# Prompt attention of a hybrid decoder step as one pipeline across units, the cache copies paced from later on, and a ring buffer with a fourth slot

## Chip, cores and metric

One Trainium2 chip, one of its cores. The metric is the time of one execution on the device in microseconds (us). TensorE (PE, its weight loads PEld), VectorE (DVE), ScalarE (ACT), GpSimd (POOL) and SyncE (SP) each work through their own queue in order; SP, POOL and ACT also issue DMAs.

## The reference, cut to what matters

One layer of a decoder runs over a prompt of 1024 rows and 64 sample rows (8 streams of 8), with shared weights. Branch A is a gated depthwise convolution of width 31, branch B dilated window attention in 3 groups of 8 heads; the groups' outputs are weighted by the softmax of their denominators. The sample rows attend to caches, and the caches are also returned, shifted by 8 rows.

```
h = x @ w_in + b_in      # [conv value | conv gate | z_a | q | k | v (3 groups each) | z_b | g_a | g_b]
c = silu(layernorm(causal_conv31(a_val * sigmoid(a_gate)) + conv_b))
for g, (window, d) in enumerate(((128, 1), (512, 4), (2048, 16))):
    o[g], lse[g] = softmax_attention(q[g], k[g], v[g])     # keys t, t-d, ..., t-window, ALiBi penalty
attn = sum_g softmax_g(lse)[g] * o[g]
m = sigmoid(g_a) * (c * silu(z_a)) @ w_a + sigmoid(g_b) * (attn * silu(z_b)) @ w_b
y = layernorm(alpha * x + m @ w_out)
outputs: y, the groups' new k and v of the prompt, the sample caches shifted by 8 rows, the conv state
```

## The kernel before

Every projection is a sum of three products: x and the weights are split into a high and a low part (`split`, lines 100 and 101: ACT writes `hi`, DVE writes `lo`, from a `raw` that SP loads), and L171 multiplies hi by hi, hi by lo and lo by hi, in column chunks of 384, 352 and 352. One 128-column slice of weights is 72 such products. `raw`, `hi` and `lo` have two buffers each. The values' projection (`project_v`, L269) works on 512 columns, from weights `vhi` and `vlo` in four pieces of 512 KB.

**Prompt attention** runs over 12 units, one for each pair of heads f (0 to 3) and group g (0 to 2). `project_qk` of unit u+2 and `project_v` are written between units; a timeline simulation inside the scheduler sets each engine's order, by priorities. A unit is cut into bursts (4, 3 or 2 by group, 36 in all). For a burst PE computes scores S (L322, 4 or 8 products on half of the array's rows), DVE adds the bias and takes the row extremum (L332), ACT takes the exponential P in place (L349), PE transposes P in blocks of 128 (L359), DVE and ACT copy the transposes out of PSUM (L367, L365), PE multiplies them with the values (O, L376, on half of the array's columns), and the result is copied to `og` (L394, L392). The first transpose of a burst waits for its last exponential, and the first score of a burst for the last reduction of the burst before. Between a unit's bursts PE is given projection products.

After each f, `combine` makes the weights of the three groups: small DVE operations, a transpose on PE (L435), a store to DRAM on POOL (`wd`), six loads that spread its rows over the partitions (`wb`, POOL, L444), and multiplications on DVE (L446, L448, L449). The convolution (`conv`, L495 and L497 on DVE) has low priority.

**Copies.** The shifted caches are 88 copies from DRAM to DRAM, issued by ACT: 64 of 1020 KB, then 16 of 1008 KB, then 8 of 480 KB. `pace` issues them after the split of a weight, `credit[1]` copies for each: 1.7 from `project_qk(0)` on, 0 in the sample stage, 1.25 after it. 74 of them are issued in the prompt phase, 14 in the stage of the last gates.

**Sample stage.** Four passes load keys and values of the caches (8, 4 and 1 loads of 512 KB for keys, as many for values) through a ring of slots `kvs`: 0, 1, 2, and from pass 0's values on also 9, 10, 11 (six). Scores are L619, L627 and L631 (the last: group 0's keys, one load `g1k`), values L664, L672 and L678. 24 gate projections (L709) are spread over this and the next stage, and stored to DRAM (`sgb`, `sga`, `sza`). Slots 9 to 11 hold `og` of the last f until its `combine` has read them; slot 5 holds keys of a unit.

**Late stages.** After the convolution's normalisation and the projection of z_b, `w_b` (8 weights of 256 KB) is multiplied; meanwhile `sza` comes back in 24 pieces through two buffers `sb` (L808), each multiplied on DVE (L827) and split into the x slots by ACT and DVE; `w_a` needs all of them. Then w_a, w_out (L875) and the last layer norm.

## Time and profile before

| | |
|---|---|
| median of 3 runs | 1440.72 us (1439.12 to 1442.24) |
| the profiled execution | 1443.81 us |
| its span on the core | 1441.8 us |
| mean granted TensorE clock | 0.991 |
| PE busy | 1408.4 us (98%) |
| DVE, ACT, POOL busy | 843.0 us (58%), 447.0 us (31%), 173.2 us (12%) |
| DMA | 280.19 MB, mean 194 GB/s |

The span is what the profiler sees between the first and the last instruction; the profiled execution is 2 us longer than its span. Times of the rows below are from the span's start. A row of a timeline merges instructions that follow each other; "x8" counts records, and a score, value or transposing product has two records. "[0.25 <-issue]" is idle time ahead of the row, and what ended it.

### The profile page before, as it was taken

What the parts mean: (1) busy time and instruction counts of PE and PEld (TensorE: products, weight loads), DVE (VectorE), ACT (ScalarE), POOL (GpSimd) and SP (SyncE); (2) the same over time, 40 slices, a digit from 0 to 9 for tenths busy, and PEclk for the clock granted to TensorE, in tenths of its full rate; (3) what the DMA queues carried; (4) which work ended last, traced back from release to release, by engine and by line L of the source; (5) the groups of instructions that cost most, each with busy time, mean ns of one, the idle gap of its engine ahead of it and who ended that gap; (6) DMA issues with size and microseconds to landing.
All of it is one profiled execution on the core that took longest, in us unless ns stands there. A gap on an engine that the chain in (4) does not pass through costs nothing.

```text
span 1441.8 us, 22039 instructions
## 1 busy us (share of the span) xinstructions
PE 1408.4 (98%) x8656; PEld 1265.2 (88%) x8656; DVE 843.0 (58%) x1642; ACT 447.0 (31%) x997; POOL 173.2 (12%) x310
## 2 busy tenths in 40 slices
PE   8899999999999999998989999999999999999997
PEld 7788888899999999988877878897899999999885
DVE  4114132328959779497986886671357326535676
ACT  5205032133424434246421211212146422203210
POOL 1011111210111011103440601100000000000000
PEclk9999999999999999999999999999999999999999
DMA  7959477365666575753477665557854326535321
GB/s 249 325 191 339 154 254 257 100 206 169 201 220 195 172 227 177 229 193 113 141 243 268 254 253 210 195 201 307 300 190 145 130 71 200 176 91 166 106 101 59
DMA packets 91590, 280.19 MB, mean 194 GB/s; under 512 B 21632, under 2 KB 47552, under 8 KB 90080
## 3 DMA queue, kind: packets, MB, share of 16 engines
q1 hardware_dynamic: 76032, 151.62, 31.5%
q10 hardware_dynamic: 2816, 87.30, 17.3%
q0 software_dynamic: 12640, 39.88, 8.6%
q8 instruction: 68, 1.11, 0.3%
q14 instruction: 34, 0.28, 0.1%
HBM read 240.85 MB, written 125.20 MB: 254 GB/s over the span
## 4 chain that ended last, share of the span: by engine, by line
PE 44%; DMA 6%; DVE 2%; issue 0%; SPq 0%; ACT 0%; DVEq 0%
PE mm L171 32%; PE mm L875 7%; DMA sb<-sza 2%; DMA kv<-in_g2v_dram 2%; PE S L619 1%; DMA kv<-in_g1v_dram 1%; DMA raw<-in_w_in_dram 1%; DMA kv<-in_g1k_dram 1%; PE S L631 1%; PE S L627 1%; PE O L678 1%; DVE x L101 1%; PE O L664 0%; PE O L376 0%; DVE lo L101 0%
## 5 line engine op out<-in xcount | busy, mean ns | idle before, releaser
L171 PE MATMUL mm<-x,hi 128*128 128x352 f32 (+1 forms) x3648 | 915.8, 331 | 7.3 <-ACT x L100 4.8
L171 PEld LDWEIGHTS mm<-x,hi 128*128 128x128 f32 x3648 | 644.7, 189 | 37.6 <-issue 24.6
L171 PE MATMUL mm<-x,lo 128*128 128x352 f32 (+1 forms) x1824 | 602.1, 330 | 0.4 <-DVE lo L101 0.4
L171 PEld LDWEIGHTS mm<-x,lo 128*128 128x128 f32 x1824 | 343.6, 188 | 15.0 <-issue 13.0
L495 DVE SCALAR_TENSOR_TENSOR cv<-ub,conv_w,cv 128x1024 f32<-128x1024 f32 x240 | 307.7, 1282 | 1.9
L101 DVE TENSOR_TENSOR lo<-raw,hi 128x1024 fp32r<-128x1024 f32 (+2 forms) x87 | 98.8, 1135 | 130.1 <-ACT hi L100 130.1
L100 ACT ACTIVATE hi<-raw 128x1024 fp32r<-128x1024 f32 (+2 forms) x87 | 85.9, 987 | 251.5 <-PE mm L171 211.4
L269 PE MATMUL mm<-vhi,x 128*128 128x512 f32 x384 | 120.2, 393 | 5.4 <-ACT vhi L100 5.4
L349 ACT ACTIVATE P<-P,st 128x128 f32<-128x128 f32 (+1 forms) x192 | 84.2, 440 | 62.8 <-DVE st L332 62.4
L269 PEld LDWEIGHTS mm<-vhi,x 128*128 128x128 f32 x384 | 72.9, 190 | 20.9 <-ACT vhi L100 5.8
L709 ACT ACTIVATE gst<-mm,b_in 128x352 f32<-128x352 f32 (+1 forms) x72 | 40.1, 558 | 143.6 <-PE mm L171 114.9
L269 PE MATMUL mm<-vlo,x 128*128 128x512 f32 x192 | 75.3, 392 | 0.0
L270 DVE TENSOR_TENSOR vst<-mm,vb 128x512 f32<-128x512 f32 x24 | 16.6, 691 | 100.3 <-PE mm L269 100.3
L497 DVE SCALAR_TENSOR_TENSOR cv<-keep,conv_w,cv 128x64 f32<-128x64 f32 x240 | 68.8, 286 | 3.5
L332 DVE CUSTOM_DVE_ANT_0 P<-S,bias 128x128 f32<-128x128 f32 (+1 forms) x192 | 55.2, 350 | 22.8 <-PE S L322 22.8
L610 POOL COPY qf<-keep 64x16 f32<-64x16 f32 x96 | 55.9, 594 | 48.5 <-PE S L619 30.0
L875 PE MATMUL mm<-wol,mh 128*128 128x512 f32 (+1 forms) x144 | 56.1, 390 | 0.0
L875 PE MATMUL mm<-woh,mh 128*128 128x512 f32 (+1 forms) x144 | 56.1, 390 | 0.0
L875 PE MATMUL mm<-woh,ml 128*128 128x512 f32 (+1 forms) x144 | 56.0, 389 | 0.0
L359 PE MATMUL PT<-ident,P 128*128 128x128 f32 x280 | 41.8, 284 | 3.9 <-ACT P L349 3.9
L269 PEld LDWEIGHTS mm<-vlo,x 128*128 128x128 f32 x192 | 36.3, 189 | 7.7 <-issue 0.2
L100 ACT ACTIVATE vhi<-raw 128x1024 fp32r<-128x1024 f32 x12 | 12.7, 1057 | 93.1 <-PE mm L277 69.3
(184 smaller groups left out, 1311.6 us busy)
## 6 DMA issues: line engine op xcount, KB each, us to landing
out_nb_dram<-in_cache_dram ACTq DMA_DIRECT2D x64, 1020.0 KB
raw<-in_w_in_dram SPq DMA_DIRECT2D x67, 512.0 KB
kv<-in_g3k_dram SPq DMA_DIRECT2D x32, 512.0 KB
kv<-in_g3v_dram SPq DMA_DIRECT2D x32, 512.0 KB
out_nb_dram<-in_cache_dram ACTq DMA_DIRECT2D x16, 1008.0 KB
kv<-in_g2k_dram SPq DMA_DIRECT2D x16, 512.0 KB
kv<-in_g2v_dram SPq DMA_DIRECT2D x16, 512.0 KB
raw<-in_w_v_dram SPq DMA_DIRECT2D x12, 512.0 KB
```

What stands on the lines that cost most here:

```text
L100: h = act.activation(out=dst_hi, in_=src, func=AF.Copy)
L101: dve.tensor_tensor(out=dst_lo, in0=src, in1=dst_hi.bitcast(F32), op=ALU.subtract)
L171: pe.matmul(ps[:, :cn], a, b, start=(i == 0), stop=(i == len(ops) - 1))
L269: pe.matmul(ps, a, b, start=(i == 0), stop=(i == len(ops) - 1))
L332: last = dve.tensor_tensor_reduce(out=pr[:, h, c], in0=ps[:, h, c], in1=bias[:, h, b0:b0 + nk], scale=-1.0, scalar=3e38, op0=ALU.add, op1= ...
L349: ex = act.activation(out=pr[:, h, c], in_=pr[:, h, c], func=AF.Exp, scale=-1.0, bias=st[:, t, h, 0:1], accum_out=st[:, t, h, 1:2])
L359: m = pe.transpose(pp[:, i * P:(i + 1) * P], pr[:, h, c:c + P], ident)
L495: dve.scalar_tensor_tensor(out=acc[:, :NP_], in0=ub[:, j:j + NP_], scalar=w, in1=acc[:, :NP_], op0=ALU.mult, op1=ALU.add)
L497: dve.scalar_tensor_tensor(out=accs, in0=us[:, :, j:j + 8], scalar=w, in1=accs, op0=ALU.mult, op1=ALU.add)
L610: pool.tensor_copy(out=qfull(g)[hs, f].rearrange("p (r j h) -> p r j h", r=4, j=4)[:, :, :, 2 * f + h2], in_=qs[hs, g * 4 + f, 16 * pr:16 ...
L709: act.activation(out=st[:, c0:c0 + cn], in_=ps, func=func, bias=b_sb[:, f:f + 1])
L875: pe.matmul(ps[:n], a, b, start=(i == 0), stop=(i == len(ops) - 1))
```

## The change

It has three parts.

- **The row.** `visit` takes the place of the loop over bursts. Each call writes, at priority 700, one row: the transposes of the newest burst, the values of the burst before that, and the scores of the next burst. The values' and the scores' first product wait, by an added dependency, for the exponential that the transposes wait for too; the values also wait for the copy out of PSUM on ACT. The pipeline is not emptied between units; two calls after the last unit empty it. What follows a unit's last value (the copy to `og`, the store of its statistics) is written with the values.
- **The copies.** `credit[1] = 1.7` moves behind `project_qk(0)`, `project_qk(1)` and `project_v(0)`. The queue of copies is the same, so ten of them move from the prompt phase to later.
- **The ring.** `kvs` begins with slots 0, 1, 2 and 5, and has seven slots later.

```diff
+    pipe = []
+    def visit(burst=None):
+        with tc.high_priority(700):
+            gate = pipe[-1]["exp"] if pipe else None
+            if pipe and "pts" not in pipe[-1]:
+                transposes(pipe[-1])
+            if len(pipe) == 2 or burst is None:
+                values(pipe.pop(0), gate)
+            if burst:
+                scores(burst, gate)
+                pipe.append(burst)
+    def together(m, gate):
+        tc.add_manual_dep(m.ins, gate.ins.name, SYNC, reason="the row starts complete")
...
+                m = pe.matmul(ps[:, h, off[t]:off[t] + nb * P], q[hs, qc], k[hs, kc], start=True, stop=True)
+                if gate is not None:
+                    together(m, gate)
+                    gate = None
...
+                if i0 + i == 0:
+                    together(m, x["exp"])
...
+                    if first:
+                        together(m, x["evac"])
+                        if gate is not None and gate is not x["exp"]:
+                            together(m, gate)
+                        first = False
...
-                    with tc.high_priority(100):
-                        m = pe.matmul(ps[:, h, off[t]:off[t] + nb * P], q[hs, qc], k[hs, kc], start=True, stop=True)
-                    if last is not None:
-                        tc.add_manual_dep(m.ins, last.ins.name, SYNC, reason="the burst starts complete")
...
-        made = scores(BURSTS[g][0])
-        for bi, burst in enumerate(BURSTS[g]):
-            off, pr = made
-            if bi + 1 < len(BURSTS[g]):
-                made = scores(BURSTS[g][bi + 1])
...
+        un = {"g": g, "q": q, "k": k, "vt": vt, "scr": scr, "bias": bias, "st": st, "og": og, "tiles": qtiles(g)}
+        for b in BURSTS[g]:
+            visit({"unit": un, "tiles": b})
+        return og, st if g == 0 else scr
...
-    credit[1] = 1.7
...
     project_v(0)
+    credit[1] = 1.7
...
+    visit()
+    visit()
...
-    kvs = [0, 1, 2]
+    kvs = [0, 1, 2, 5]
```

The new lines of the same work are L331 (scores), L360 (transposes), L384 (values), L341 (reduction), L348 (exponential), L368 and L366 (copies of the transposes), L454 (transpose in `combine`), L465, L467 and L468 (its multiplications), L514 and L516 (convolution), L652 (scores of group 0's cache).

How the order moves is read at four places. **First, PE in the middle of a unit** of group 0 (mm are projection products, S scores, PT transposes, O values; "waits" names the engines waited for). Before:

```order
2342 L171 MATMUL mm_4149<-x_122,hi_4117 128x352
2343 L322 MATMUL S_3920<-qkv_3120,qkv_3119 128x256 [waits DVE_49]
2344 L322 MATMUL S_3920<-qkv_3120,qkv_3119 128x256 x3
2345 L171 MATMUL mm_4149<-x_130,hi_4117 128x352
2346 L359 MATMUL PT_3935<-ident_197,P_3889 128x128 [waits PE_49,Activation_49]
2347 L359 MATMUL PT_3935<-ident_197,P_3889 128x128
2348 L376 MATMUL O_3877<-PT_3894,vt_3836 64x128 [waits DVE_49]
2349 L376 MATMUL O_3877<-PT_3894,vt_3836 64x128 x7
2350 L359 MATMUL PT_3935<-ident_197,P_3889 128x128 x2
2351 L359 MATMUL PT_3941<-ident_197,P_3889 128x128 x4
2352 L171 MATMUL mm_4149<-x_122,lo_4118 128x352
```

The same place after:

```order
2332 L171 MATMUL mm_4108<-x_122,hi_4076 128x352
2333 L360 MATMUL PT_3872<-ident_197,P_3862 128x128 [waits PE_49,Activation_49]
2334 L360 MATMUL PT_3872<-ident_197,P_3862 128x128 x3
2335 L360 MATMUL PT_3878<-ident_197,P_3862 128x128 [waits DVE_49]
2336 L360 MATMUL PT_3878<-ident_197,P_3862 128x128 x3
2337 L384 MATMUL O_3884<-PT_3834,vt_3791 64x128 [waits DMAHW7_49,PE_49]
2338 L384 MATMUL O_3884<-PT_3834,vt_3791 64x128 x5
2339 L331 MATMUL S_3891<-qkv_3078,qkv_3077 128x256 [waits DVE_49]
2340 L331 MATMUL S_3891<-qkv_3078,qkv_3077 128x256 x3
2341 L171 MATMUL mm_4108<-x_130,hi_4076 128x352
```

Scores, transposes and values stood in separate groups, cut by each other and by projection products; now they stand in one row, the scores last. Over the whole program PE changes between its array shapes 257 times before and 226 times after, and 34 to 57 projection products stand between the scores of one row and the transposes of the next.

**Second, DVE at the third combine**, where its multiplications wait for `wb`. Before:

```order
680 L495 SCALAR_TENSOR_TENSOR cv_5228<-ub_5050,conv_w_203,cv_5228 128x1024 [waits DVE_49]
681 L446 TENSOR_TENSOR attn_5292<-og_3841,wb_5475 128x1024 [waits DMASW5_49,DMASW4_49]
682 L495 SCALAR_TENSOR_TENSOR cv_5228<-ub_5050,conv_w_203,cv_5228 128x1024 [waits DVE_49]
683 L448 TENSOR_TENSOR wb_5479<-og_4459,wb_5479 128x1024 [waits DMASW7_49,DMASW6_49]
684 L495 SCALAR_TENSOR_TENSOR cv_5228<-ub_5050,conv_w_203,cv_5228 128x1024 [waits DVE_49]
685 L332 ISA P_5704,st_5679<-S_5699,bias_5677 128x256 [waits PE_49]
```

After:

```order
691 L514 SCALAR_TENSOR_TENSOR cv_5183<-ub_5005,conv_w_203,cv_5183 128x1024 [waits DVE_49]
692 L465 TENSOR_TENSOR attn_5247<-og_3796,wb_5434 128x1024 [waits DMASW5_49,DMASW4_49]
693 L467 TENSOR_TENSOR wb_5438<-og_4418,wb_5438 128x1024 [waits DMASW7_49,DMASW6_49]
694 L514 SCALAR_TENSOR_TENSOR cv_5183<-ub_5005,conv_w_203,cv_5183 128x1024 [waits DVE_49]
695 L101 TENSOR_TENSOR lo_6324<-raw_6321,hi_6323 128x1024 [waits DMAHW5_49,PE_49,Activation_49]
696 L468 TENSOR_TENSOR attn_5247<-attn_5247,wb_5438 128x1024 [waits DVE_49]
697 L499 SCALAR_TENSOR_TENSOR ub_5872<-mm_5969,b_in_195,ub_5872 128x384 [waits DMASW1_49,PE_49]
698 L514 SCALAR_TENSOR_TENSOR cv_5183<-ub_5005,conv_w_203,cv_5183 128x1024 [waits DVE_49]
699 L368 COPY PT_5688<-PT_5689 128x512 [waits PE_49]
700 L467 TENSOR_TENSOR wb_5443<-og_4728,wb_5443 128x1024 [waits DMASW1_49,DMASW0_49]
701 L341 ISA P_5715,st_5638<-S_5710,bias_5636 128x256 [waits PE_49]
```

The multiplication that waits for `wb` stands ahead of the reductions of a burst in both. On PE 42 projection products stood between the combine's transpose and the scores of that burst; after, 36 stand between it and the scores of the burst before that one, and 45 more until this row.

**Third, PE in sample pass 0** around the transpose of the last combine (L435, now L454; k2 is L627 with 128x32 shapes, k1 L631, now L652). Before:

```order
3522 L171 MATMUL mm_6474<-x_122,hi_6339 128x352
3523 L171 MATMUL mm_6474<-x_130,hi_6339 128x352
3524 L171 MATMUL mm_6474<-x_122,lo_6340 128x352
3525 L435 MATMUL PT_6306<-ident_197,w_6290 48x128 [waits DVE_49]
3526 L171 MATMUL mm_6474<-x_123,hi_6339 128x352
3527 L627 MATMUL S_6208<-kv_6241,qf_693_6162 32x256 [waits DMAHW1_49,Pool_49]
3528 L627 MATMUL S_6208<-kv_6241,qf_693_6162 32x256 x3
```

After:

```order
3603 L171 MATMUL mm_6688<-x_124,lo_6633 128x352
3604 L652 MATMUL S_6198<-kv_6255,qf_693_6152 128x256 [waits DMAHW4_49]
3605 L652 MATMUL S_6198<-kv_6255,qf_693_6152 128x256 x3
3606 L454 MATMUL PT_6296<-ident_197,w_6280 48x128 [waits DVE_49]
3607 L171 MATMUL mm_6722<-x_117,hi_6718 128x384 [waits Activation_49]
```

Before, the combine's transpose stood 73 rows ahead of the k1 scores (row 3598); after, it follows them.

**Fourth, ACT in the w_b stage** (hi with 128x512 is a w_b weight, x a split of a `sza` piece, out_nb a copy). Before:

```order
637 L100 ACTIVATE hi_10318<-raw_10316 128x512 [waits DMAHW0_49,PE_49]
638 L709 ACTIVATE gst_10175<-mm_10234,b_in_195 128x352 [waits PE_49]
639 L100 ACTIVATE x_10701<-sb_10713 128x352 [waits DVE_49]
640 L100 ACTIVATE x_10718<-sb_10720 128x384 [waits DVE_49]
641 L100 ACTIVATE hi_10373<-raw_10371 128x512 [waits DMAHW2_49,PE_49,Activation_49]
```

After:

```order
627 L100 ACTIVATE hi_10310<-raw_10308 128x512 [waits DMAHW7_49,PE_49]
628 L137 DMA out_nb_dram<-in_cache_dram 16x7680 [waits DMAHW6_49]
629 L137 DMA out_nb_dram<-in_cache_dram 16x7680
630 L730 ACTIVATE gst_10165<-mm_10225,b_in_195 128x352 [waits PE_49]
631 L100 ACTIVATE x_10701<-sb_10713 128x352 [waits DVE_49]
632 L100 ACTIVATE x_10718<-sb_10720 128x384 [waits DVE_49]
633 L100 ACTIVATE hi_10367<-raw_10365 128x512 [waits DMAHW2_49,PE_49,Activation_49]
634 L137 DMA out_nb_dram<-in_cache_dram 16x7680 [waits DMAHW5_49]
```

The late queue of copies is 24 long after, against 14: one of 1008 KB and all eight of 480 KB now stand on the splits of w_b, where none stood before.

## Rows read from the trace of the kernel before

**Rows 1.** The profile page, part 1: busy time and share of each engine.

```profile
PE 1408.4 (98%) x8656; PEld 1265.2 (88%) x8656; DVE 843.0 (58%) x1642; ACT 447.0 (31%) x997; POOL 173.2 (12%) x310
```

**Rows 2.** Windows of the span: start and end, length, then busy time (and instructions) of PE, PEld, DVE, ACT, POOL, the granted TensorE clock, the share of DMA engines busy, GB/s. The first two lie in the first `project_v`, the third behind the third combine, the last two in the late stages.

```profile
57.70:62.26 4.56, 4.56 (x21) 3.57 (x20) 0.00 (x0) 0.00 (x0) 0.00 (x0) 1.00 1.01 358
67.80:71.58 3.78, 3.78 (x9) 2.99 (x10) 1.20 (x1) 1.65 (x3) 1.30 (x2) 0.54 1.53 538
...
669.60:675.50 5.90, 5.90 (x32) 5.18 (x33) 5.90 (x14) 2.70 (x4) 2.27 (x6) 0.50 0.48 137
...
1090.00:1155.00 65.00, 65.00 (x392) 64.31 (x391) 36.28 (x40) 36.79 (x47) 1.59 (x3) 1.00 0.34 114
1190.00:1240.00 50.00, 48.02 (x287) 46.81 (x286) 34.80 (x70) 15.10 (x30) 0.54 (x1) 1.00 0.67 207
```

**Rows 3.** PE and its weight loads in a burst of a group 0 unit, timeline: start, length, engine, line, operation, shapes, records.

```profile
476.20 0.33 PE L171 MATMUL mm<-x,lo 128*128 128x384 f32 x1
...
476.38 0.34 PE L171 MATMUL mm<-x,hi 128*128 128x384 f32 x1
476.64 0.73 PEld L322 LDWEIGHTS S<-qkv,qkv 64*128 64x128 f32 x8 [0.25 <-issue]
476.65 1.13 PE L322 MATMUL S<-qkv,qkv 64*128 64x256 f32 x8
477.71 0.64 PEld L376 LDWEIGHTS O<-PT,vt 128*64 128x64 f32 x12 [0.33 <-issue]
...
478.51 0.86 PEld L359 LDWEIGHTS PT<-ident,P 128*128 128x128 f32 x8 [0.17 <-issue]
```

**Rows 4.** The first `project_v`, timelines of ACT (ACTq: its queue issuing DMAs) and of PE.

```profile
38.39 1.16 ACTq L137 DMA_DIRECT2D out_nb_dram<-in_cache_dram  x2
...
53.05 1.06 ACT L100 ACTIVATE vhi<-raw 128x1024 fp32r<-128x1024 f32 x1 [6.28 <-DMA raw<-in_w_v_dram]
...
66.69 1.06 ACT L100 ACTIVATE vhi<-raw 128x1024 fp32r<-128x1024 f32 x1 [10.66 <-DMA raw<-in_w_v_dram]
...
62.03 0.39 PE L269 MATMUL mm<-vlo,x 128*128 128x512 f32 x1
67.80 1.65 PE L269 MATMUL mm<-vhi,x 128*128 128x512 f32 x3 [5.38 <-ACT vhi L100]
```

**Rows 5.** DMA queues from 20 to 66 us: packets, MB, share of 16 engines' time (q10 carries the copies, q1 SP's loads).

```profile
q10 hardware_dynamic: 256, 8.36, 49.7%
q1 hardware_dynamic: 2822, 4.15, 29.4%
```

**Rows 6.** The third combine, timelines of PE, DVE and ACT.

```profile
645.24 0.27 PE L435 MATMUL PT<-ident,w 128*48 128x128 f32 x1
...
656.26 1.23 DVE L446 TENSOR_TENSOR attn<-og,wb 128x1024 f32<-128x1024 f32 x1 [3.54 <-DMA wb<-wd]
...
667.58 1.28 ACT L349 ACT_TABLE_LOAD   x1
668.87 0.51 ACT L349 ACTIVATE P<-P,st 128x256 f32<-128x256 f32 x1
...
669.53 1.12 PE L359 MATMUL PT<-ident,P 128*128 128x128 f32 x4 [3.92 <-ACT P L349]
```

**Rows 7.** Scores and last exponential of two ordinary bursts, timelines of PE and ACT (a burst of four score products, and one of eight).

```profile
612.39 0.93 PE L322 MATMUL S<-qkv,qkv 64*128 64x128 f32 x8
...
615.94 0.49 ACT L349 ACTIVATE P<-P,st 128x256 f32<-128x256 f32 x1
...
523.65 1.16 PE L322 MATMUL S<-qkv,qkv 64*128 64x128 f32 x16
...
530.83 0.39 ACT L349 ACTIVATE P<-P,st 128x128 f32<-128x128 f32 x1
```

**Rows 8.** The k1 scores of pass 0: the chain of waits (start, length, what), POOL's and SP's timelines, PE's timeline, and the same scores in pass 1.

```profile
727.27 11.18 DMA kv<-in_g1k_dram
...
726.72 2.10 POOL L444 DMA_DIRECT2D wb<-wd  x4 [0.43 <-DMA wd<-PT]
...
728.72 0.33 SPq L587 DMA_DIRECT2D kv<-in_g3v_dram  x1
...
738.49 3.78 PE L631 MATMUL S<-kv,qf 128*128 128x256 f32 x8 [3.74 <-DMA kv<-in_g1k_dram]
...
811.86 1.89 PE L631 MATMUL S<-kv,qf 128*128 128x256 f32 x8
```

**Rows 9.** Waits of PE for value loads from 745 to 1000 us: who, for what: us in total, times, longest us.

```profile
PE O L678 <- DMA kv<-in_g1v_dram: 1.9, 2, 1.3
...
PE O L664 <- DMA kv<-in_g3v_dram: 1.0, 2, 0.8
```

**Rows 10.** The chain of waits from 1150 to 1330 us, by line, and its longest piece; waits of DVE in the same stretch; stores of `sza` (count, KB each, median us to landing) from 1027 to 1155 us, where copies run, and from 1155 to 1190 us, where none does.

```profile
by line: PE mm L171 70.2%; DMA sb<-sza 16.1%; DVE x L101 4.1%; issue 2.9%; DVE sb L827 2.3%; DVE lo L101 2.0%; ACT x L100 1.2%; DVE tf L818 1.1%; DVEq L818 0.1%; DVEq L827 0.1%; DVEq L101 0.0%
...
1239.92 90.16 PE mm L171 x545
...
DVE sb L827 <- DMA sb<-sza: 19.7, 17, 2.9
...
sza<-gst POOLq DMA_DIRECT2D x6, 544.0 KB, 5.8
...
sza<-gst POOLq DMA_DIRECT2D x1, 544.0 KB, 3.5
```

More of the change, by code (lines that the diff above doesn't have):

```diff
@@ new lines, in scores @@
+    def scores(x, gate):
+        un = x["unit"]
+        g, q, k, st, tiles = un["g"], un["q"], un["k"], un["st"], un["tiles"]
+        off, n = {}, 0
+        for t in x["tiles"]:
+            off[t] = n
+            n += tiles[t][2] * P
+        ps = s_ps()
+        for t in x["tiles"]:
+            qc, kc, nb, _ = tiles[t]
+            for h in range(2):
+                hs = slice(64 * h, 64 * h + 64)
+                m = pe.matmul(ps[:, h, off[t]:off[t] + nb * P], q[hs, qc], k[hs, kc], start=True, stop=True)
+                if gate is not None:
+                    together(m, gate)
+                    gate = None
+        pr = half("P", [P, 2, 512], 2)
+        for t in x["tiles"]:
+            nk = tiles[t][2] * P
+            b0 = 0 if g == 2 else 256 - nk
+            c = slice(off[t], off[t] + nk)
+            for h in range(2):
+                dve.tensor_tensor_reduce(out=pr[:, h, c], in0=ps[:, h, c], in1=un["bias"][:, h, b0:b0 + nk],
+                                         scale=-1.0, scalar=3e38, op0=ALU.add, op1=ALU.min,
+                                         accum_out=st[:, t, h, 0:1])
+        blocks = []
+        for t in x["tiles"]:
+            c = slice(off[t], off[t] + tiles[t][2] * P)
+            for h in range(2):
+                x["exp"] = act.activation(out=pr[:, h, c], in_=pr[:, h, c], func=AF.Exp, scale=-1.0,
+                                          bias=st[:, t, h, 0:1], accum_out=st[:, t, h, 1:2])
+                blocks += [(t, h, j, off[t] + j * P) for j in range(tiles[t][2])]
+        x["pr"], x["blocks"] = pr, blocks
@@ new lines, in transposes @@
+    def transposes(x):
+        blocks = x["blocks"]
+        pts = half("PT", [P, 8, P], 2)
+        for i0 in range(0, len(blocks), 4):
+            part = blocks[i0:i0 + 4]
+            pp = pt_ps()
+            for i, (t, h, j, c) in enumerate(part):
+                m = pe.transpose(pp[:, i * P:(i + 1) * P], x["pr"][:, h, c:c + P], ident)
+                if i0 + i == 0:
+                    together(m, x["exp"])
+            src = pp[:, :len(part) * P]
+            dst = pts[:, i0:i0 + len(part)].rearrange("p a b -> p (a b)")
+            if i0:
+                x["evac"] = act.activation(out=dst, in_=src, func=AF.Copy)
+            else:
+                dve.tensor_copy(out=dst, in_=src)
+        x["pts"] = pts
```

127 lines of the change are left out of this document (39 added, 88 removed).

## The prediction

> **What bounds the kernel now.** The page's busy times come first: PE is busy 1408.4 of 1441.8 us [rows 1], so only PE's own gaps, its slow stretches and the cost between its groups can be won; work moved on other engines counts only where PE waits for it. The windows come next: in three places the granted clock falls from 1.00 to about 0.5 behind a stall, that is from 2.4 to 1.2 GHz [rows 2]. Then, place by place, the timelines and waits that show what PE waited for: the value weights in the first `project_v` [rows 4, 5], an exponential behind the third combine [rows 6], the load `g1k` of sample pass 0 [rows 8], value loads of the later passes [rows 9]. Last, the chain of waits of the w_b stage, where it leaves PE for the loads of `sza` and comes back at 1239.92 [rows 10]; there DMA sets the end, and the change adds DMAs there.
>
> All terms are made against the profiled execution, 1443.8 us, 3.1 us above the median of 1440.72; the same difference is then put to the median.
>
> **1. Copies away from the first values.** Before, eight copies were issued among the weights of the first two projections and the values; from 20 to 66 us they hold 49.7% of the DMA engines' time, and the loads of SP 29.4% [rows 5]. The third and fourth value weights make ACT wait 6.28 and 10.66 us, and PE waits 5.38 us at 67.80 [rows 4]. What follows runs at half clock: nine products from 67.80 to 71.58 take 3.78 us, where 20 intervals take 4.56 us before, 0.228 us each, 2.05 us for nine; 1.7 us lost [rows 2]. After, the order of ACT has all four value splits ahead of the first copy. PE needs 48 products of 0.228 us, 11 us, for one value weight, so a load of 512 KB has 11 us of cover, and the copies that held half of the engines' time beside it are gone. **-7.1 us**; if the next stall is a part of it, -5.
>
> **2. Fewer changes of shape.** A projection product stands 0.18 us behind the one before (476.20 to 476.38), but the first score 0.27 us behind the last product (476.38 to 476.65), and the weight loads wait 0.17 to 0.33 us at each such change for nothing the profile shows [rows 3]. So a change between array shapes costs some 0.09 us of PE. The order has 31 fewer of them: 31 x 0.09 = **-2.8 us**. Ends: -2 (some gap stays inside a row) and -4.
>
> **3. The third combine.** DVE waits 3.54 us for `wb` at 656.26, 11.0 us after the transpose at 645.24; the reductions of the next burst stand behind it, ACT reloads a table for 1.28 us, and the last exponential starts at 668.87; PE waits 3.92 us [rows 6]. Then 5.9 us run at half clock [rows 2]; in the share of the first stall, 1.7 of 3.78, that loses 2.7 us. After, 81 projection products and a row, not 42, lie between that transpose and the scores whose reductions stand behind `wb`: 81 x 0.165 (545 products in 90.16 us, [rows 10]) and some 4 us of the row make 17 us, so `wb` has landed when they come. **-6.6 us**. But the same kind of wait appears at other places, under 4.
>
> **4. The rows' gate.** Each row starts when the exponential of the newest burst is done, and transposes, values and scores are then all held by it, with every product behind them on PE. What covers it: 34 to 57 products between the scores and the next row, 5.6 to 9.4 us at 0.165 us. What has to fit: from the scores' end to the exponential's end 3.1 us (613.3 to 616.4) for a burst of four products, 6.4 us (524.8 to 531.2) for one of eight [rows 7]. Most rows fit. Those that don't by these numbers: the first combine, whose `wb` wait stands ahead of the reductions of a row only 36 products behind its transpose. Transpose, 36 products and a row put the scores' end 11.3 us behind it; `wb` comes after 11.0 us or up to 2 us later, then two multiplications of 1.23 us [rows 6], a copy of transposes and what a burst of eight takes, 9.5 us in all, end at 20.5 to 22.5; the next row stands 57 products behind, at 20.7. That is 0 to 2 us, and some rows of eight products lose tenths. **+3 us**; ends 0 and +7 (a stall of 3.9 us with its half clock).
>
> **5. The load of g1k.** It took 11.18 us, beside four `wb` loads and a value load issued in the same two microseconds; PE waited 3.74 us and its eight records then took 3.78 us, against 1.89 us in pass 1 [rows 8]. After, the combine's transpose, and so `wb`, comes behind these scores, and the ring is one slot longer. 3.74 + 1.89 = **-5.6 us**. If value loads alone still delay it, a third of it stays.
>
> **6. The other loads of the sample stage.** PE waits 1.9 and 1.0 us for values [rows 9]. Seven slots let loads run one further ahead; but slots 9 to 11 are freed by the last combine, which comes later against pass 0's values. Its last read of them falls 20 to 25 us behind the transpose (11 to 16 us for `wb`, then some seven operations of DVE of 1.2 us), a load follows, and PE reaches the values 163 products, 28 us, behind it. **-1.5 us**; ends -2.9 (all gone) and +5 (pass 0 waits once, with its half clock).
>
> **7. Late copies.** Fifteen of the 24 late copies are beside gate weights, where 0.34 of the DMA time is used and PE waits for nothing [rows 2]: nothing, unless the weights come 10 us late. Nine stand on the splits of w_b, one of 1008 KB ahead of the stage and eight of 480 KB in it. There the DMA engines are busy 0.67 of the time [rows 2], and of 180 us of the chain 16.1%, 29 us, are loads of `sza`; PE waits for them at the end, so what they lose is lost one for one [rows 10]. A store of `sza` takes 5.8 us beside copies and 3.5 us without [rows 10], so 2.3 us is the upper price of a copy for a transfer that meets it: 8 x 2.3 = 18, and 1 us for the issues on ACT, whose splits lie on the same chain. The lower end is 0: two loads are in flight, and a copy may fall on the one that isn't on the chain. I take a third, **+6 us**, since only half of the loads are on the chain and a copy doesn't meet each.
>
> The Trainium skill ("DMA: Bandwidth & Descriptors", section "Queues, rings and completion order") says that each DMA engine goes round between the queues that have work, a packet at a time, so that a load waits for one packet of a copy and not for the copy. The copies of rows 5 hold an engine 1.4 us for each packet; by that rule the price would end at 8 x 1.4 = 11 us, and the sum at 1431 us. No row here shows how the packets alternate.
>
> **The sum.** -7.1 - 2.8 - 6.6 + 3 - 5.6 - 1.5 + 6 = -14.6 us: 1429.2 us on the profiled execution, **1426 us** on the median.
>
> **The rivals.**
>
> *The copies pay back their whole price.* If each of the eight copies delays the chain of `sza` by the full 2.3 us, the term is +19 and not +6: 1439 us, within 0.2% of before. For it: the chain sets that stage's end already. Against: in the prompt phase SP's loads ran beside copies of twice the size and PE waited only in the first `project_v`.
>
> *The gate stalls every row* (the slower one). Place: the 36 rows' heads. Mechanism: scores at the row's end make reductions and exponentials begin late, and everything of the row waits for the last of them; a burst of eight needs 6.4 us [rows 7] and the cover begins at 5.6. Price: 36 x the mean wait. From 0.5 us a row it takes back 18 us and the kernel is no faster; at 0.7 us it is 25 us in place of 3, 1448 us. For it: no row's head has a second chance, as before with three groups each held by its own condition. Against: before, PE waited once for an exponential in 36 bursts [rows 6], and bursts of four need only 3.1 us.
>
> *One of the three stalls moves and doesn't vanish.* In pass 0 the four key loads that go first must land within 32 products after the last scores free slot 5, 5.5 us; or g1k is late again behind value loads. A stall of 3.7 us and 2 to 3 us of half clock: 1432 us.
>
> *The change does only the shapes* (the stalls are made again one stage later): -2.8 + 3, 1441 us.
>
> *Better than forecast.* Rows never wait, copies are hidden: 1426 - 3 - 6 - 1.4 = 1416 us.
>
> **How the numbers follow.** Forecast 0.50; better 0.12; a moved stall 0.15; copies at full price 0.08; only shapes 0.04; stalling rows 0.11. 1426 is the likeliest. Faster by over 0.2% (below 1437.8; 0.2% is about what a measurement of this kernel can tell from no change) gathers forecast, better, moved stall and part of the copies' case: 0.80. The same: 0.08. Slower: stalling rows and a mixture of full copies with a moved stall, 0.12. The range must reach from better with 4 us to spare to the copies' full price: 1412 to 1440; about 0.15 lies above it, 0.03 below.
>
> **What would show it.** Right: PE has no wait for `vhi` near 62 us and no clock below 1 there; no wait for an exponential near 665 us; the g1k load lands in about 5 us; the clock falls only at the end; PE waits a little more in the w_b stage for `sza`. Wrong: waits "<-ACT P" at the transposes (L360) in many rows, or a fall of the clock in the prompt phase; DMA loads of `sza` well above 3 us with PE idle before the first w_a product for over 10 us; waits for key loads at the first L640 scores of pass 0.

## The result, and the profile after

The changed kernel takes 1432.38 us (median of 7 runs, 1424.39 to 1434.50) where the kernel before takes 1440.72 (7 runs, 1438.07 to 1442.24): a ratio of 0.9932, interval 0.9909 to 0.9955, or 8.3 us less. That is faster, within the range, and 6 us above the forecast of 1426. The profiled execution took 1428.53 us, with a span of 1426.7, so 15.3 us below the profiled one of before (14.6 was forecast). This is the first profile of the changed kernel; e5 below is a second one.

The page, part 1, of the changed kernel (answers [rows 1]):

```profile
PE 1400.8 (98%) x8656; PEld 1266.4 (89%) x8656; DVE 843.2 (59%) x1642; ACT 448.6 (31%) x997; POOL 157.8 (11%) x310
```

PE does the same 8656 instructions in 7.6 us less busy time. A matmul at half clock and one that stands behind a change of shape both count as busy, so part of the gain is inside "busy". The windows of the changed kernel, with the columns of [rows 2]:

```profile
62.26:71.58 9.32, 9.32 (x43) 7.72 (x42) 1.38 (x2) 0.00 (x0) 1.08 (x2) 1.00 0.38 147
669.60:675.50 5.90, 5.90 (x54) 5.25 (x55) 5.90 (x15) 4.70 (x12) 1.00 (x2) 1.00 0.61 187
...
1164.50:1214.50 50.00, 44.51 (x255) 43.01 (x254) 27.19 (x55) 11.42 (x22) 0.54 (x1) 0.97 0.78 255
1207.00:1210.40 3.40, 3.40 (x11) 3.40 (x12) 1.80 (x5) 0.18 (x1) 0.00 (x0) 0.51 0.90 276
1234.30:1237.70 3.40, 3.17 (x9) 2.90 (x10) 3.19 (x7) 1.23 (x2) 0.00 (x0) 0.51 0.07 13
```

Two of the half-clock stretches of before, at 67.80 and 669.60, are at 1.00 now. In the w_b stage (here from 1164.50, since it begins 24.8 us earlier) PE is busy 44.51 of 50 us and the DMA share is 0.78; the stage of before had 48.02 and 0.67 [rows 2]. Two stretches of half clock have come there.

Three marks of PE's records tell the rest. The first score product starts at 109.14 us (116.76 before): 7.6 us won at the first values. The first product of w_b starts at 1164.53 (1189.34): 24.8 us won by then. The first product of w_out starts at 1319.72 (1334.85): 15.1. **The w_b stage gives back 9.7 us.** It takes 155.2 us from one mark to the next, and 145.5 before. "The w_b stage" means these two marks in all that follows.

The first `project_v`, ACT's timeline (answers [rows 4]): the value weights are waited for at most 1.89 us.

```profile
42.38 1.06 ACT L100 ACTIVATE vhi<-raw 128x1024 fp32r<-128x1024 f32 x1 [1.89 <-DMA raw<-in_w_v_dram]
```

A row of the pipeline, PE's timeline (answers [rows 3]): transposes, values and scores stand side by side, with projections behind.

```profile
470.86 1.03 PE L360 MATMUL PT<-ident,P 128*128 128x128 f32 x8
471.82 0.88 PE L384 MATMUL O<-PT,vt 128*64 128x128 f32 x12
472.63 1.13 PE L331 MATMUL S<-qkv,qkv 64*128 64x256 f32 x8
```

The row behind the third combine, timelines of DVE, ACT and PE (answers [rows 6]): the reductions still stand behind a multiplication by `wb`, and ACT still reloads its table (1.28 us), but the last exponential ends 0.24 us before the row begins, and PE doesn't wait.

```profile
657.60 1.22 DVE L467 TENSOR_TENSOR wb<-og,wb 128x1024 f32<-128x1024 f32 x1
658.73 0.42 DVE L341 CUSTOM_DVE_ANT_0 P<-S,bias 128x256 f32<-128x256 f32 x1
...
662.02 0.50 ACT L348 ACTIVATE P<-P,st 128x256 f32<-128x256 f32 x1
...
662.76 1.04 PE L360 MATMUL PT<-ident,P 128*128 128x128 f32 x8
```

The waits of PE from 100 to 700 us and then from 700 to 1000 us (who, for what: us in total, times, longest):

```profile
PE PT L360 <- ACT P L348: 0.8, 2, 0.5
...
PE S L648 <- DMA kv<-in_g2k_dram: 2.0, 2, 1.8
PE S L640 <- DMA kv<-in_g3k_dram: 0.4, 1, 0.4
PE O L685 <- DMA kv<-in_g3v_dram: 0.2, 1, 0.2
```

Two rows wait, for less than 1 us together. The k1 products of pass 0 don't wait (3.7 before, [rows 8]); two other key loads of that pass do. The value loads are almost waited for no more (2.9 before, [rows 9]).

The w_b stage, chain of waits from 1160 to 1240 us, its shares and some of its loads of `sza` (answers [rows 10]):

```profile
by line: DMA sb<-sza 52.2%; PE mm L171 16.8%; DVE x L101 9.2%; issue 4.9%; DVE sb L848 4.8%; DVE lo L101 3.3%; DVE tf L839 3.3%; DMA PT<-sgb 2.4%; ACT x L100 1.9%; SPq L113 0.7%; DVEq L839 0.4%; DVEq L848 0.2%; SPq L829 0.0%
...
1167.85 6.57 DMA sb<-sza
1199.25 5.96 DMA sb<-sza
...
1231.06 2.27 DMA sb<-sza
```

And the waits of DVE from 1150 to 1330 us:

```profile
DVE sb L848 <- DMA sb<-sza: 33.6, 20, 4.3
```

52.2% of 80 us is 41.8 us of the chain, where before had 16.1% of 180, 29.0 us [rows 10]; DVE waits 33.6 us for them, 19.7 before. The eight copies of 480 KB are sent between 1165 and 1198 us, and most of the longest loads are there (up to 6.57 us); the last, without a copy beside it, takes 2.27 us.

### The profile page after: what moved, and what is told of

Its sections match the earlier page's. It is cut to its first block, busy times and chain, and to the rows that moved or that the text cites. A ratio compares the mean times of both kernels' runs of the same rounds, so it can differ in the third digit from the quotient of the medians.

```text
span 1426.7 us, 22026 instructions
## 1 busy us (share of the span) xinstructions
PE 1400.8 (98%) x8656; PEld 1266.4 (89%) x8656; DVE 843.2 (59%) x1642; ACT 448.6 (31%) x997; POOL 157.8 (11%) x310
## 4 chain that ended last, share of the span: by engine, by line
PE 43%; DMA 5%; DVE 3%; issue 0%; SPq 0%; ACT 0%; DVEq 0%
PE mm L171 31%; PE mm L896 7%; DMA sb<-sza 3%; DMA kv<-in_g2k_dram 1%; PE O L685 1%; DMA cv<-cvd 1%; PE S L640 1%; DVE cv L514 1%; PE O L693 1%; PE S L648 1%; DVE x L101 1%; PE S L652 0%; PE O L699 0%; DMA kv<-in_g3v_dram 0%; DVE sb L848 0%
## 5 line engine op out<-in xcount | busy, mean ns | idle before, releaser
L171 PE MATMUL mm<-x,hi 128*128 128x352 f32 (+1 forms) x3648 | 916.6, 331 | 7.2 <-ACT x L100 7.2
L171 PEld LDWEIGHTS mm<-x,hi 128*128 128x128 f32 x3648 | 645.5, 189 | 42.1 <-issue 28.9
L171 PE MATMUL mm<-x,lo 128*128 128x352 f32 (+1 forms) x1824 | 601.1, 330 | 0.4 <-DVE lo L101 0.4
L171 PEld LDWEIGHTS mm<-x,lo 128*128 128x128 f32 x1824 | 343.7, 188 | 12.9 <-issue 10.8
L514 DVE SCALAR_TENSOR_TENSOR cv<-ub,conv_w,cv 128x1024 f32<-128x1024 f32 x240 | 306.6, 1278 | 1.9
L348 ACT ACTIVATE P<-P,st 128x128 f32<-128x128 f32 (+1 forms) x192 | 84.2, 441 | 70.1 <-DVE st L341 69.5
L516 DVE SCALAR_TENSOR_TENSOR cv<-keep,conv_w,cv 128x64 f32<-128x64 f32 x240 | 67.7, 282 | 3.3
L341 DVE CUSTOM_DVE_ANT_0 P<-S,bias 128x128 f32<-128x128 f32 (+1 forms) x192 | 54.9, 345 | 10.6 <-PE S L331 10.6
L631 POOL COPY qf<-keep 64x16 f32<-64x16 f32 x96 | 41.5, 444 | 29.5 <-PE S L640 14.6
L368 DVE COPY PT<-PT 128x512 f32<-128x512 f32 x36 | 24.6, 684 | 27.4 <-PE PT L360 26.1
```

The source lines that it names most:

```text
L171: pe.matmul(ps[:, :cn], a, b, start=(i == 0), stop=(i == len(ops) - 1))
L341: dve.tensor_tensor_reduce(out=pr[:, h, c], in0=ps[:, h, c], in1=un["bias"][:, h, b0:b0 + nk], scale=-1.0, scalar=3e38, op0=ALU.add, op1=A ...
L348: x["exp"] = act.activation(out=pr[:, h, c], in_=pr[:, h, c], func=AF.Exp, scale=-1.0, bias=st[:, t, h, 0:1], accum_out=st[:, t, h, 1:2])
L368: dve.tensor_copy(out=dst, in_=src)
L514: dve.scalar_tensor_tensor(out=acc[:, :NP_], in0=ub[:, j:j + NP_], scalar=w, in1=acc[:, :NP_], op0=ALU.mult, op1=ALU.add)
L516: dve.scalar_tensor_tensor(out=accs, in0=us[:, :, j:j + 8], scalar=w, in1=accs, op0=ALU.mult, op1=ALU.add)
```

## Experiments

Theory A, from these rows: the copies beside `sza` are the give-back; the gain ahead of it is four things added (the first values, the changes of shape, the third combine, the loads of pass 0), and the last depends on a few microseconds, so it should vary from run to run. Rivals: the give-back belongs to the stage's new place in time, and not to the copies; the fourth slot has nothing to do with pass 0; the rows' waits cost, and don't earn. The kernels were timed in three groups (e1 to e4, e5 to e8, e9 to e11); those of a group share a chip and the runs of the kernel before, whose medians are 1445.24, 1444.71 and 1445.70 us. The expected times of e1 to e4 come from the 1440.72 and 1432.38 us above, so the ratios to the kernel before say more than the times: the changed kernel's is 0.9932 above and 0.9926 in e5. No run of e1 to e4 or e9 to e11 has the changed kernel beside it. Stages, waits and windows are of one profiled execution for each kernel.

**e1: no late copy beside `sza`.**

```diff
-    credit[1] = 1.25
+    credit[1] = 2.0
```

> The changed kernel, with late copies paced at 2.0 in place of 1.25 for each weight, so that all 24 are issued on gate and z_b weights and none on w_b. Theory A (the copies beside the loads of sza cost what the w_b stage gives back): from the first w_b product to the first w_out product 145 to 148 us in place of 155, no half clock there, and 1423 to 1427 us in all. Rival B (the stage is longer because the order put the last sza pieces later): 153 to 156 us, no change in the total, 1430 to 1434. Rival C (copies cost the same wherever they lie in the late stages): the gates' stage is longer by what w_b wins, 1430 to 1434.

Measured: 1429.37 us (1427.30 to 1432.92), ratio 0.9893 (0.9874 to 0.9912). All 24 late copies are sent by 1149 us, ahead of the stage, which takes 146.4 us, with no half clock. The time is above the 1423 to 1427 us of theory A, but the kernel before was slower too: 0.9893 of 1440.72 is 1425. Chain of waits from 1160 to 1240 us:

```profile
by line: DMA sb<-sza 36.6%; PE mm L171 31.8%; DVE x L101 7.9%; DVE sb L848 6.1%; issue 5.9%; DVE lo L101 4.6%; ACT x L100 3.2%; DVE tf L839 3.1%; SPq L829 0.5%; DVEq L839 0.4%; DVEq L848 0.1%
```

36.6% of 80 us is 29.3 us, what it was before the change. The copies are the give-back: 8.8 us for eight of 480 KB, 1.1 us each. Rival B, the order, has it at 153 us or more and fails. Eight more copies beside the gate weights cost nothing that shows there (rival C): from the output of the sample passes to the first w_b product it takes 148.3 us with 16 copies (the changed kernel) and with 24 (e1); before, with 14, it took 147.4.

**e2: the early copies where they were.**

```diff
+    credit[1] = 1.7
     todo = []
...
     project_v(0)
-    credit[1] = 1.7
```

> The changed kernel with the copies paced from the first projection on again (rows and ring as changed). Theory A: the stall of 5.4 us and its half clock come back at the first value weights (+7.4), and the w_b stage gets back its 9.7 us: 1428 to 1431 us. Rival B (order, not copies, makes the w_b stage longer): 1438 to 1441 us.

Measured: 1438.48 us (1435.35 to 1441.26), ratio 0.9951 (0.9932 to 0.9969). The stage is 145.4 us, and the wait for the values is back, so the mechanism of theory A holds and that of rival B doesn't, although the time lies where rival B had it. Waits of PE from 50 to 760 us:

```profile
PE S L640 <- DMA kv<-in_g3k_dram: 5.7, 1, 5.7
PE mm L269 <- ACT vhi L100: 4.3, 1, 4.3
```

The time is above what theory A expected by waits that the changed kernel doesn't have: 5.7 us for a g3k load of pass 0, and 2.4 us behind the second combine (L171 for DVE's L499), each with a lower clock behind it (0.57 on the mean from 724 to 730 us, 0.51 from 517.7 to 521).

**e3: the copies moved in the kernel before.** The same two lines of `credit[1] = 1.7`, moved as the change moves them, and nothing else.

> The kernel before with the move of the copies alone. Theory A: -7.4 us at the first value weights, +7 to +10 at w_b: 1440 to 1444 us, no gain from this part by itself. Rival B (the w_b stage loses through the rows' order): 1432 to 1434 us.

Measured: 1448.27 us (1444.63 to 1453.16), ratio 1.0021 (1.0007 to 1.0036). The first score comes at 109.6 us, 7.2 earlier, the stage takes 158.0 us, 12.5 longer, in the old order of PE: again the copies, not the order. Alone, this part costs 3 us, the upper end of theory A. Eight copies cost 1.6 us each here, more than in e1. The wait at the third combine shrinks to 1.0 and 1.4 us in two rows (3.9 before), and another of 3.2 us comes behind the second combine; a timeline of PE and then a window behind it:

```profile
527.49 0.92 PE L322 MATMUL S<-qkv,qkv 64*128 64x256 f32 x6 [3.23 <-DVE st L332]
```

```profile
527.50:533.50 6.00, 6.00 (x40) 5.57 (x41) 6.00 (x11) 2.23 (x12) 0.00 (x0) 1.00 0.01 1
```

The clock stays at 1.00 behind it.

**e4: three ring slots in the changed kernel.**

```diff
-    kvs = [0, 1, 2, 5]
+    kvs = [0, 1, 2]
```

> The changed kernel with the ring of 0, 1, 2 (later six slots). Theory A (the wait for g1k went because the combine's transpose, and with it wb, comes behind it): within 3 us of the changed kernel, no wait over 1.5 us at the k1 scores of pass 0. Rival (the fourth slot took the wait away): a wait of 3 to 4 us and half clock at k1, 1437 to 1440 us.

Measured: 1445.01 us (1441.54 to 1452.57), ratio 1.0000 (0.9981 to 1.0018): the slot is worth 0.7%, some 10 us, beside the other parts. Each theory is half right: there is no wait at k1 (theory A), but the whole gain goes (the rival), by a wait at another place. PE's wait, SP's queue (its DMA issues), and a wait of that queue (690 to 730 us):

```profile
722.57 1.94 PE L640 MATMUL S<-kv,qf 128*32 128x512 f32 x8 [7.59 <-POOL qf L631]
...
695.56 7.28 SPq L608 DMA_DIRECT2D kv<-in_g3k_dram  x4
713.08 0.33 SPq L113 DMA_DIRECT2D raw<-in_w_in_dram  x1
713.51 0.37 SPq L608 DMA_DIRECT2D kv<-in_g3k_dram  x1
...
SPq L113 <- DVE lo L101: 12.8, 2, 10.2
```

The wait is at the last k3 products, not at k1. The profile names a copy of queries on GpSimd, but the queries of these products were copied by 664 us; what they lacked is the g3k load issued at 713.51, whose last packet lands at 722.4. Its slot was free at 709.0, when the products before had read it; the load stood in SP's queue behind a weight load, which waited 10.2 us, to 713.1, for DVE to have read a weight's buffer. In the changed kernel all four loads of this stretch go out from 694.89 in 2.3 us:

```profile
694.89 2.30 SPq L608 DMA_DIRECT2D kv<-in_g3k_dram  x4
```

**e5: the changed kernel again.** (What the expectation calls the first gate product is the first product of w_b.)

> The changed kernel itself, timed beside the three kernels of this call, as their yardstick, with a second look at the loads of the first sample pass. Theory A (a DMA bound first pass, in which it is a matter of a few us which key load the matrix engine waits for): the ratio to the kernel before lies again near 0.993 (0.990 to 0.996), and the single waits of the first pass differ from those of the first look by a microsecond or more, while those of the prompt stage and the waits beside the copies on the gate weights (some 155 us from the first gate product to the first output product) come back the same. Rival (the whole program drifts, not the first pass): the waits of all stages differ by as much.

Measured: 1432.89 us (1431.59 to 1435.01), ratio 0.9926 (0.9907 to 0.9944), 11.8 us below the kernel before. The profiled run, 1433.92 us, was 5.4 us slower than the first one. Rows wait 1.6 us in all (0.8), the stage takes 156.2 us (155.2). By the first w_b product it is 20.4 us ahead of before, not 24.8. Waits of PE from 700 to 1000 us:

```profile
PE S L648 <- DMA kv<-in_g2k_dram: 2.7, 2, 2.5
PE O L685 <- DMA kv<-in_g3v_dram: 1.0, 1, 1.0
```

And a window just behind the longer of the two g2k waits:

```profile
718.80:722.20 3.40, 3.40 (x17) 2.20 (x17) 3.40 (x10) 0.00 (x0) 1.44 (x4) 0.51 0.78 294
```

A wait for the same load of 2.5 us in place of 1.8, and here the clock falls behind it. PE's 8656 products stand in the same order in both profiles, so their starts can be compared one by one: of the 5.4 us, 2.0 arise here, 1.0 at a g3v load of the next pass, 0.9 at the waits of rows, 1.0 in the w_b stage, and the small rest at other places. So the ratio came back, and this stretch has the largest part, but the single waits of pass 0 differ by 0.7 us at the most, not by 1 or more, and the prompt and the w_b stage differ too: theory A isn't shown against its rival.

**e6: the rows alone.** The changed kernel with `credit[1] = 1.7` at its old place and `kvs = [0, 1, 2]`.

> The one pipeline of rows alone: the cache copies at their old place and three ring slots, as before. Theory A (the parts add up to the whole: copies moved alone cost about 3 us, the fourth slot is worth about 10, so the rows are what is left): 2 to 4 us below the kernel before; no wait of 6 us at the third combine, the V product wait of about 5 us beside the copies still there, and a wait of 5 us or more for a key load of the first sample pass. Rival 1 (the rows are worth the shape changes alone): 0 to 2 us below. Rival 2 (the rows carry most of the gain, and ring and copies only matter together with them): 8 us or more below.

Measured: 1439.61 us (1435.98 to 1447.33), ratio 0.9977 (0.9961 to 0.9994), 3 to 5 us below before, as theory A had it. Waits of PE from 640 to 760 us:

```profile
PE S L640 <- DMA kv<-in_g3k_dram: 2.3, 2, 2.1
PE PT L360 <- ACT P L348: 1.4, 1, 1.4
```

The waits at the third combine (3.9 us) and at k1 (3.7) are gone without ring and copies; smaller ones stand at other places, one of 2.4 us behind the second combine as in e2. The wait for the values stayed (5.7 us), as expected; a wait of 5 us or more for a key load of pass 0 isn't there.

**e7: the ring alone.** The kernel before with `kvs = [0, 1, 2, 5]`.

> The kernel before with the fourth ring slot alone. Theory A (the slot is what takes the key load waits of the first pass away, whatever stands ahead of it): 5 to 10 us below the kernel before, no wait of 5 us at the k1 group of the first pass, nor one of over 4 us at its k3 group. Rival (as the prediction's step 5 had it, the load is late since the combine's transposed weights come late, and the slot alone has nothing to do with it): 0 to 2 us below, with the wait of 5.6 us at k1 still there.

Measured: 1439.12 us (1437.61 to 1444.44), ratio 0.9972 (0.9959 to 0.9985), 4 to 5.6 us below before, at the lower end of theory A and outside the rival's range. The same view:

```profile
PE PT L359 <- ACT P L349: 3.9, 1, 3.9
PE S L627 <- POOL qf L610: 3.3, 1, 3.3
```

The third combine waits as before, k1 doesn't; k2 does, for 3.3 us. So a slot or the rows each take the k1 wait away.

**e8: no gate.** The scores and values lose the wait on the exponential.

```diff
-                if gate is not None:
-                    together(m, gate)
-                    gate = None
...
-                        if gate is not None and gate is not x["exp"]:
-                            together(m, gate)
```

> The changed kernel without the waits of the scores and the values on the row's exponential; the transposes keep theirs. Theory A (the added waits cost 1.1 us in two places, and what they keep together is worth some changes of shape of 0.09 us each): within 2 us of the changed kernel in the same call, the two waits of 0.4 and 0.7 us gone or in other places, and the busy time between products of one shape and another the same or up to 2 us more. Rival (the waits are what holds the row together and so carry the gain of the rows): 4 us or more above the changed kernel. Rival (the waits cost more than their two places show): 3 us or more below it.

Measured: 1444.14 us (1441.78 to 1446.70), ratio 0.9997 (0.9984 to 1.0010), 11 us above the changed kernel of e5. The first rival holds. Costliest groups of PE by shape from 106 to 640 us (busy us, mean ns of one), first of the kernel before, then of the changed one, then of this one:

```profile
L359 PE MATMUL PT<-ident,P 128*128 128x128 f32 x232 | 33.5, 279 | 0.0
L376 PE MATMUL O<-PT,vt 128*64 128x128 f32 x448 | 30.9, 279 | 0.0
L322 PE MATMUL S<-qkv,qkv 64*128 64x256 f32 x160 | 22.8, 400 | 0.0
L322 PE MATMUL S<-qkv,qkv 64*128 64x128 f32 x160 | 12.7, 290 | 0.0
```

```profile
L384 PE MATMUL O<-PT,vt 128*64 128x128 f32 x448 | 30.9, 279 | 0.0
L360 PE MATMUL PT<-ident,P 128*128 128x128 f32 x232 | 30.3, 273 | 0.8 <-ACT P L348 0.8
L331 PE MATMUL S<-qkv,qkv 64*128 64x256 f32 x160 | 22.8, 400 | 0.0
L331 PE MATMUL S<-qkv,qkv 64*128 64x128 f32 x160 | 12.4, 288 | 0.0
```

```profile
L381 PE MATMUL O<-PT,vt 128*64 128x128 f32 x448 | 32.4, 280 | 0.0
L357 PE MATMUL PT<-ident,P 128*128 128x128 f32 x233 | 31.5, 276 | 0.0
L331 PE MATMUL S<-qkv,qkv 64*128 64x256 f32 x160 | 25.9, 403 | 0.0
L331 PE MATMUL S<-qkv,qkv 64*128 64x128 f32 x160 | 13.4, 292 | 0.0
```

The sums are 99.9, 96.4 and 103.2 us. Counted in PE's records from 106 to 660 us, the kind of product (projection, scores, transposes, values) changes 203, 162 and 208 times. Transposes and projections have the same array shape; by array shape, over the whole run, it changes 278, 248 and 291 times. Without the gate the scheduler places each kind of product by its own operands, and projections come between; the row exists because of the gate. The edit changes the scheduler's order as well as the waits, so it doesn't tell one from the other. These groups hold 6.8 of the 11 us; where the rest lies isn't settled. The 11 us are more than the rows gain alone (3 to 5 us, e6).

**e9: e1 once more**, as the yardstick of the next two kernels.

> The changed kernel with two copies to each weight set after the sample passes where it has five to four, once more, as the yardstick of the two kernels beside it. Expected again: a ratio to the kernel before near 0.9893 (0.987 to 0.992), 146 to 147 us from the first gate product on to the first output product.

Measured: 1425.22 us (1421.39 to 1431.91), ratio 0.9865 (0.9837 to 0.9894), just below the 0.987 to 0.992 that was expected; the stage takes 146.3 us. With e1, this is the best kernel of the study, 1.1 to 1.4% below before.

**e10: queries on ScalarE**, in e9's kernel.

```diff
-                    pool.tensor_copy(
-                        out=qfull(g)...
+                    if pr == 0 and g == 1:
+                        act.activation(out=o, in_=i, func=AF.Copy)
+                    else:
+                        pool.tensor_copy(out=o, in_=i)
```

> That kernel, with the eight copies of the first sample pass that lay out the queries of the second head group made by ScalarE in place of GpSimd. Theory A (in the first pass GpSimd's 24 copies stand between the last combine's steps and the key products, and the k2 products wait for them or for the loads behind them in turn): the wait of 2 to 3 us at the first k2 product and the half clock behind it go or shrink to under 1 us, 3 to 6 us below the yardstick. Rival (the key loads land no earlier, so the wait stays and only its releaser changes): within 2 us of the yardstick. Rival (ScalarE's queue, with the copies of the cache and the exponentials on it, is late itself): slower by 2 us or more.

Measured: 1430.05 us (1425.07 to 1440.09), ratio 0.9892 (0.9865 to 0.9919): not below the yardstick, and the intervals overlap. The k2 products of pass 0 no longer wait (1.2 us in e9), but the last k3 products wait 1.6 us for g3k and the first values of pass 0 3.8 us for `snew`; two more waits in the prompt phase (5.5 and 3.5 us) were in this profiled run, the slowest of the seven. Inconclusive: the wait moved, and whether GpSimd was its cause isn't shown.

**e11: more late copies.** `credit[1] = 1.0` in place of 1.25.

> The changed kernel with one copy to each weight set after the sample passes in place of five to four, so that more of the 24 late copies (11 or 12 by the count of weight sets, in place of 8) are sent beside the small stores and loads of the second gate product. Theory A (each copy there costs the loads on the chain about as much): 157 to 161 us from the first gate product on to the first output product, 2 to 6 us above the changed kernel (so 1434 to 1439 where the kernel before takes 1444). Rival (the price is one of the stage's first loads alone, paid once by the eight that are there already): 155 us again, within 1 us of the changed kernel.

Measured: 1439.00 us (1434.35 to 1446.06), ratio 0.9958 (0.9939 to 0.9978). Eleven copies are sent from 1178 us on, where the stage begins at 1177.6, and one some 12 us ahead. The stage takes 159.4 us, 13.0 more than e9 without copies, and the time is 3.7 to 4.6 us above the changed kernel by the ratios: theory A. But the eleven are not alike. DMA issues from 1177 to 1236 us (count, KB each):

```profile
out_nb_dram<-in_cache_dram ACTq DMA_DIRECT2D x3, 1008.0 KB
out_nb_dram<-in_cache_dram ACTq DMA_DIRECT2D x6, 480.0 KB
```

The last two of 480 KB are sent at 1259.8 and 1265.9, when the last load of `sza` has landed (1249.2) and PE sets the pace again. So 6.0 MB stand beside the chain here, against 3.9 MB in the changed kernel: 13.0 and 8.8 us are 2.2 us for each MB in both, while the price of a copy would be 1.5 us (of nine) against 1.1. But the same eight copies make 2.5 us for each MB in e5 and 3.2 in e3, so these profiles show that more copies cost more, and not whether number or size sets the price. The profiled run also had a row's gate that waits. DVE waits for the second combine's statistics, the reductions of a burst stand behind it, and PE waits. Timelines of DVE and PE, and then a window of the 6.8 us behind it, at half clock:

```profile
456.40 0.18 DVE L441 TENSOR_TENSOR mn<-mn,stn 128x16 f32<-128x16 f32 x1 [7.30 <-DMA stn<-scr]
464.33 0.28 DVE L341 CUSTOM_DVE_ANT_0 P<-S,bias 128x128 f32<-128x128 f32 x1
...
466.63 1.54 PE L360 MATMUL PT<-ident,P 128*128 128x128 f32 x6 [3.64 <-ACT P L348]
```

```profile
465.60:472.40 6.80, 5.77 (x31) 4.29 (x32) 6.76 (x10) 2.85 (x7) 0.00 (x0) 0.50 0.12 31
```

In the first profile of the changed kernel the same load made DVE wait 3.2 us, and PE didn't wait. So the gate has a price in some runs, set by one small load.

## Why the prediction was right in its mechanism and half off in size

Each term stands with what was forecast and what was found.

- **1, first values: -7.1; found -7.6** (e3: -7.2, and back in e2). Right, in place and size.
- **2, changes of shape: -2.8; found -2.7 to -3.5**. By array shape, as forecast, the records have 30 changes fewer (278 to 248): 30 x 0.09 = 2.7. The groups under e8 give 3.5; their busy times overlap at each end (the transposes of the row above end at 471.89, the values begin at 471.82), so this is the upper end.
- **3, third combine: -6.6; found gone**, wait and half clock. The rows alone suffice (gone in e6, there in e7); the copies alone bring it to 1.0 and 1.4 us at full clock (e3). The forecast had `wb` landed with room; in fact the exponential ends 0.24 us ahead of the row.
- **4, the rows' gate: +3; found +0.8** in the first profile and 1.6 in the second (1.0 to 2.2 in e1, e2, e4 and e9). The size was too high for these, but its mechanism, reductions behind a combine's wait, is what e11's profiled run shows with 3.64 us and 6.8 us of half clock. Its working also puts the scores' end 11.3 us behind the transpose, where 36 products and some 4 us of a row make 10.2; by that the wait came to 1 to 3 us, not 0 to 2. What the step left out is what the gate earns: without it the changes of shape come back (e8).
- **5, g1k: -5.6; found gone.** The reason given was one of two that suffice (e6 and e7). What the step missed is where the ring is worth its 10 us: at the key loads ahead of k1, with the late copies (e4).
- **6, other sample loads: -1.5.** Found -0.3 in the first profile and +2 in the second; this step was mis-sized. Value loads gave 2.7 us (1.9 in the second), but key loads took 2.4 in the first, and 2.7 in the second, with a fall of the clock that costs another 1.3 by the starts of PE's products. The rival "one of the three stalls moves", with its four key loads of pass 0, is this in part, at half its price.
- **7, late copies: +6; found +9.7 and, in the second profile, +10.7.** The step that failed most. I let a third of the upper price stand because only some loads are on the chain; in fact eight copies cost 8.8 us (e1), 1.1 us each and not 0.75, with two stretches of half clock, and 12.5 us in the order of before (e3). The Trainium skill ("DMA: Bandwidth & Descriptors", section "Queues, rings and completion order") says that the engines alternate between queues packet by packet; with 1.4 us for a packet, the prediction has eight copies at 11 us at the most by it, close to what was measured. But the 1.4 us is no packet's time: of the 256 packets in [rows 5] half carry 4 bytes, the others 65,280 bytes, and these take 2.9 us. A copy of 480 KB has 16 packets of 30,720 bytes (and as many of 4 bytes), which take 1.49 us in the changed kernel's trace, so the number was nearly right by luck. Eight times 1.49 us are 12 us, which e3's 12.5 us slightly exceeds. No run shows how the packets alternate, so that the rule is the cause is only argued.

On the profiled execution the sum was -14.6 and -15.1 was found by the end of PE's work, since term 7 was 4 us too small and the gain ahead of it (24.8 us, 20.6 forecast) as much larger: that the two errors cancel is luck. Terms 1 to 3, 5 and 6, with the gate's 0.8 us, are some 22 of the 24.8 by these numbers; the last 2 to 3 us aren't placed. On the median 8.3 us were found (11.8 in e5), less than on the profiled execution, since the profiled run of before lay above its median (1443.81 against 1440.72) and that of the changed kernel below its own (1428.53 against 1432.38). The second profile, near the median, has longer waits of the rows and of pass 0 and a longer w_b stage; its span, 1432.1, is 9.7 us below that of before. So one profiled run of each kernel was too little to put the sum to the median. Which waits make the spread of the executions isn't shown.

The parts in their combinations, as ratios to the kernel before (each known to about 0.002):

| | copies early, three slots | copies early, four | copies late, three | copies late, four |
|---|---|---|---|---|
| bursts | 1 | 0.9972 (e7) | 1.0021 (e3) | not run |
| rows | 0.9977 (e6) | 0.9951 (e2) | 1.0000 (e4) | 0.9926 (e5), 0.9932 |

Rows and ring add up with the copies early. The late copies cost 0.2% with three slots and gain about as much with four, and the ring, worth 4 to 6 us alone, is worth some 10 with rows and late copies. Both values of the ring are clear of the noise, the copies' 0.2% only alone (e3). Each part moves what pass 0 waits for; what the ring and the late copies make without the rows wasn't run.

## What to carry to other kernels

Copies that cost nothing beside large products can cost most of their own transfer time beside a chain of small stores and loads: before moving background copies, look in the chain of waits for the stage that a DMA bounds, and keep them out of it. In this program kinds of products that were put in a row stayed in a row only with one condition that held them all; its price is read where an in-order engine that feeds it waits for a small load. When a stall went, another load of the same queue was the next bound, and a load can be late because of what stands ahead of it in its queue, not for want of a slot; so parts of a change around one stage have to be timed together and apart.

## What the runs showed of the hardware that was not expected

A copy of 480 KB from DRAM to DRAM, on ACT's queue, cost a chain of `sza` loads of 176 to 192 KB on SP's queue 1.1 to 1.2 us in the changed kernel (its two profiles against e1 and e9) and 1.6 in the order of before (e3), where one of its packets takes 1.49 us, while 24 copies beside weight loads took no more time than 16. And a wait's own length is only part of its price: 2.5 us was followed by 3.4 us at 0.51 of the clock (e5), 3.64 us by 6.8 us at 0.50 (e11), but 1.83 us (the first profile) and 3.23 us (e3) by none. The longer wait isn't always the one that the clock answers.
